# Recurrence: one joint solve of the 16x16 blocks for two units in a row, on 128 partitions

## Chip, cores, metric

One core of one Trainium2 chip. The metric is the device time of one execution in microseconds, the median of the runs.

## What is computed

The program runs two small transformer stacks one after the other on 256 tokens of width 1024, in fp32. The change lies in the second stack's first mixer, in the bidirectional recurrence over 256 context and 256 latent tokens (8 heads of 64):

```
def step(S, inp):
    r, w, k, v, kk, a = inp
    S = (S * w[:, :, None, :]
         - jnp.einsum('bhvk,bhk->bhv', S, kk)[..., None] * (kk * a)[:, :, None, :]
         + v[..., None] * k[:, :, None, :])
    return S, jnp.einsum('bhvk,bhk->bhv', S, r)
...
S_cf, y_cf = wkv7_scan(S0, dir_inputs(f_ctx, 0), reverse=False)
S_cb, y_cb = wkv7_scan(S0, dir_inputs(f_ctx, 1), reverse=True)
_, y_lf = wkv7_scan(S_cf, dir_inputs(f_lat, 0), reverse=False)
_, y_lb = wkv7_scan(S_cb, dir_inputs(f_lat, 1), reverse=True)
```

The kernel does not step token by token. It takes chunks of 64 tokens, writes a chunk's effect as a 64x64 unit triangular system per head, inverts that, and carries only the state from chunk to chunk.

## The kernel before

**Units.** The list `order` in `even_mixer` (line 1100) holds eight units: a direction `d` (0 forward, 1 backward) and a tile `t` of 128 tokens, that is two chunks of 64 tokens by 8 heads. Units 0 to 3 are the context's, 4 to 7 the latent's; even units are forward, odd ones backward. Unit 2p and unit 2p+1 together let two scan steps run.

**Steps of a unit.**
- *Front* (`rwkv_in`, lines 1449 to 1493): decays and gates from the low-rank features, products into `fr` and `gh`.
- *Back* (lines 1494 to 1545): the unit's features are loaded into `fe`, which has one buffer; VectorE scales them into `ak` and `ar`; 16 products of 128 columns go into `gg` and `gh` (line 1527), VectorE masks them into `g`. Of `g` the part that is to be inverted is stored to a DRAM buffer `dq` (line 1539), for a backward unit after VectorE's transpose (line 1537, into `fe`). Eight transposes on TensorE (line 1543) are the last readers of `fe`, with that store for a backward unit.
- *Solve* (`rwkv_solve`, lines 1555 to 1567): the 64 diagonal blocks of 16x16 (2 chunks, 8 heads, 4 blocks) are read back from `dq` with one block to a partition, tile `dl` [64, 16, 16] (line 1559). 14 rounds of a product into `dt` and a sum into `dl` (both through line 120) invert them, a fill sets the diagonal (line 1566), and the result goes to a DRAM buffer `dy` (line 1567). There are four `dq` and four `dy`, used in turn.
- *Maps* (`rwkv_maps`, lines 1569 to 1656): the solved blocks are loaded as `x` (line 1588, one load a chunk), VectorE transposes them (line 1589), and two rounds of products on TensorE (line 1594), a mask on VectorE (tile `T`) and a sum into `x` extend the 16x16 inverses to 64x64. Then come the unit's maps (lines 1636 and 1650). That is 116 calls of a product, and most of them wait for the one before by way of VectorE or ScalarE.
- *Scan steps* (`rwkv_step`, lines 1668 and 1677): after an odd unit's maps, two steps of 32 products.

**Order.** The program is written in the order of the list `GA` (line 22) and then of the loop at line 1300: `b0 s0 f1 f2 b1 f3 s1` stand among the projections before the recurrence (b is back, f front, s solve, and the number the unit); then for n from 2 on come back, front and solve of unit n, n+2 and n, then the maps of unit n-2. Softmax attention of the same mixer (`even_attention`: products into `sc`, `tr`, lines 1011, 1029, 1057) is filled in between by `fill`. Gates and readout (`gates`, `readout`) are a side stream beside the maps. A scheduler of the framework turns that into one fixed order for each engine, which waits on semaphores. All the recurrence's DMAs are issued on SP's queue.

Of the kernel before, what the change touches and what calls it, by code (L numbers as in the profile page):

```python
# [12 lines left out]
F32 = mybir.dt.float32  # L13
F32R = mybir.dt.float32r
AF = mybir.ActivationFunctionType
ALU = mybir.AluOpType
# [31 lines left out]
def kernel(ctx: ExitStack, tc: tile.TileContext, A: dict, out: bass.AP, taps=None):  # L48
    nc = tc.nc
# [8 lines left out]
    def nm(s):  # L58
        uid[0] += 1
        return f"{s}_{uid[0]}"  # L60
# [22 lines left out]
    def const(name, pool=cpool, tag=None, queue=nc.sync):  # L83
        src = A[name]
        t = pool.tile(list(src.shape), F32, tag=tag or name, name=nm(name))
        queue.dma_start(out=t, in_=src)
        return t
# [31 lines left out]
    def tt(o, a, b, op):  # L119
        V.tensor_tensor(out=o, in0=a, in1=b, op=op)  # L120
# [958 lines left out]
    def even_mixer(l, en):  # L1079
        T = 512  # L1080
        close_psum()
        with tc.tile_pool(name=nm("em"), bufs=1) as pk, tc.tile_pool(name=nm("rf"), bufs=2) as fp, \
# [9 lines left out]
            C = {n: const(n, pk) for n in ("rwkv_wa", "rtri", "gmask", "tmask", "eye2", "sgn")}  # L1092
# [7 lines left out]
            order = []  # L1100
            for i, (t0, t1) in enumerate(((2, 3), (0, 1))):
                order += [dict(d=d, t=t, u=u, i=i) for u, (d, t) in enumerate(((0, t0), (1, t1), (0, t1), (1, t0)))]
            dq = [dp.tile([64, 1040], F32, tag=f"dq{n}", name=nm("dq")) for n in range(NS)]
            dy = [dp.tile([64, 1040], F32, tag=f"dy{n}", name=nm("dy")) for n in range(NS)]
# [20 lines left out]
            with tc.tile_pool(name=nm("emn"), bufs=1) as wk:  # L1125
# [5 lines left out]
                for j in range(3):  # L1131
                    z, f = en.tile("fu", 512), en.tile("fg", 512, 2)
                    tt(z, pss[j], en.rb, ALU.mult)
                    for v in range(2):
                        c = slice(v * 256, v * 256 + 256)
# [9 lines left out]
            with tc.tile_pool(name=nm("ga"), bufs=1) as ga, tc.tile_pool(name=nm("emw"), bufs=2) as wk:  # L1145
# [100 lines left out]
                    order[u].update(next(units[u]))  # L1246

                def solve(u):
                    rwkv_solve(C, order[u])

                def do_v(f):
                    vf = shifted(8 + f)
                    stage(D["v"][:, :, f * 128:(f + 1) * 128], 4, [vf[:, t * 128:(t + 1) * 128] for t in range(4)])

                do = dict(k=do_k, q=do_q, r=do_r, v=do_v, f=front, b=back, s=solve)
                for what, n in GA:
                    do[what](n)
# [3 lines left out]
            close_half(0)  # L1261
            open_psum(gg=1, m=2, y=1, sc=1, tr=1)
            rwkv(C, D, order, (front, back, solve), bon, yac)
            for cm in reversed(held):
                cm.__exit__(None, None, None)
# [180 lines left out]
    def half(i):  # L1446
        return slice(64 * i, 64 * i + 64)
# [104 lines left out]
    def lanes_of(x):  # L1552
        return x[:, 0:1024].rearrange("l (r c) -> l r c", r=16)[:, :, 0:16]

    def rwkv_solve(C, un):
        wk = C["us"]

        y = wk.tile([64, 16, 16], F32, tag="dl", name=nm("dl"), bufs=2)
        nc.sync.dma_start(out=y, in_=lanes_of(un["dq"]))
        for c in range(1, 15):  # L1560
            n = 15 - c
            tmp = wk.tile([64, 64], F32, tag="dt", name=nm("dt"), bufs=2)
            o = tmp[:, :c * n].rearrange("p (a r) -> p a r", a=c)
            tt(o, y[:, 0:c, c].unsqueeze(2).to_broadcast([64, c, n]), y[:, c, c + 1:16].unsqueeze(1).to_broadcast([64, c, n]), ALU.mult)
            tt(y[:, 0:c, c + 1:16], y[:, 0:c, c + 1:16], o, ALU.add)
        V.memset(y.rearrange("p a r -> p (a r)")[:, 0:256:17], 1.0)
        nc.sync.dma_start(out=lanes_of(un["dy"]), in_=y)

    def rwkv_maps(C, D, un):
        d, t, u, dy, ar, g = (un[n] for n in ("d", "t", "u", "dy", "ar", "g"))  # L1570
# [213 lines left out]
    with tc.tile_pool(name="fin", bufs=1) as wk:  # L1784
# [3 lines left out]
        for k in range(0, 8, 2):  # L1788
            o = en.tile("fo", 512, 4).rearrange("p (k t) -> p k t", k=2)
# [153 lines left out]
```

## Time and profile before

| | |
|---|---|
| runs | 2334.14, 2339.14, 2340.65 us; median 2339.14 |
| profiled execution | 2338.47 us, its span 2336.7 us |
| TensorE (PE) busy | 2248.5 us, 96% |
| VectorE (DVE) busy | 1571.7 us, 67%, 3080 instructions |
| ScalarE (ACT) busy | 1073.2 us, 46% |
| mean granted TensorE clock | 0.981 |

A busy TensorE is not TensorE at its peak, since matmuls are pipelined and their ends modelled. Start times below count from the span's start. The granted clock is a share of the full 2.4 GHz. The recurrence lies between about 900 and 1175 us.

### The profile page before, as it was taken

To read this page: it belongs to the slowest core of one execution; us is meant where nothing else is said; L and a number is where in the kernel's file an instruction comes from. 1 tells how busy PE (TensorE), PEld (TensorE's weight loads), DVE (VectorE), ACT (ScalarE), POOL (GpSimd) and SP (SyncE) were. 2 spreads that over 40 slices of the span, in tenths; PEclk is the share of its full clock that TensorE was granted. 3 is DMA by queue.
4 is the path that set the end of the run, shared out by engine and by line. 5 is a ranking of instruction groups with operands and counts; after the bars stand their busy time and mean duration, and the time that the engine had idled before them with its cause. 6 is when DMAs were issued, how large, how long until landed. Compare 5 with 4: busy or idle time off the path is not lost.

```text
span 2336.7 us, 35597 instructions
## 1 busy us (share of the span) xinstructions
PE 2248.5 (96%) x13714; PEld 1842.1 (79%) x13714; DVE 1571.7 (67%) x3080; ACT 1073.2 (46%) x1887; POOL 5.6 (0%) x10
## 2 busy tenths in 40 slices
PE   8999999999999998998889999999999999999998
PEld 6688787877787786776767778787778788768998
DVE  7867778766845767889578677437755334787555
ACT  6756666322224637765535222224422223476444
POOL 0000000000000000000000000000000000000000
PEclk9999999999999999899989999999999999999999
DMA  8556545655623545433254565323553222314553
GB/s 295 174 185 209 178 149 163 190 179 159 201 95 111 172 138 142 113 88 76 77 202 146 164 190 177 129 90 121 178 189 125 91 98 92 104 37 141 184 185 119
DMA packets 161945, 342.02 MB, mean 146 GB/s; under 512 B 48624, under 2 KB 76272, under 8 KB 161648
## 3 DMA queue, kind: packets, MB, share of 16 engines
q1 hardware_dynamic: 161056, 339.15, 45.7%
q8 instruction: 108, 1.77, 0.3%
q10 hardware_dynamic: 720, 0.60, 0.1%
q14 instruction: 61, 0.50, 0.1%
HBM read 321.86 MB, written 17.84 MB: 145 GB/s over the span
## 4 chain that ended last, share of the span: by engine, by line
PE 87%; DVE 6%; ACT 4%; DMA 2%; issue 1%; SPq 0%; DVEq 0%; ACTq 0%
PE mm L115 24%; PE mm L117 24%; PE mm L116 24%; PE m L1594 1%; PE tr L219 1%; PE m L1650 1%; DVE wlo L98 1%; PE po L1057 1%; PE wm L274 1%; ACT whi L97 1%; PE wm L331 1%; PE gg L1527 1%; PE po L541 1%; DMA fe<-fd 1%; PE tr L1057 0%
## 5 line engine op out<-in xcount | busy, mean ns | idle before, releaser
L97 ACT CAST whi<-raw 128x1024 fp32r<-128x1024 f32 (+2 forms) x437 | 437.0, 1001 | 961.5 <-PE mm L116 591.4
L115 PE MATMUL mm<-xh,whi 128*128 128x512 f32 (+1 forms) x1912 | 679.2, 359 | 13.3 <-ACT xh L97 6.0
L117 PE MATMUL mm<-xh,wlo 128*128 128x512 f32 (+1 forms) x1912 | 678.6, 356 | 4.5 <-DVE wlo L98 4.3
L116 PE MATMUL mm<-xl,whi 128*128 128x512 f32 (+1 forms) x1912 | 678.6, 356 | 1.3 <-DVE xl L98 1.1
L98 DVE TENSOR_TENSOR wlo<-raw,whi 128x1024 fp32r<-128x1024 f32 (+2 forms) x437 | 508.1, 1164 | 250.5 <-ACT whi L97 244.4
L115 PEld LDWEIGHTS mm<-xh,whi 128*128 128x128 f32 x1912 | 363.4, 191 | 77.5 <-ACT whi L97 16.9
L117 PEld LDWEIGHTS mm<-xh,wlo 128*128 128x128 f32 x1912 | 364.1, 191 | 57.9 <-DVE wlo L98 8.1
L116 PEld LDWEIGHTS mm<-xl,whi 128*128 128x128 f32 x1912 | 364.5, 191 | 55.4 <-DVE xl L98 4.2
L117 PE MATMUL mm<-hh,wlo 128*128 128x512 f32 (+1 forms) x704 | 260.0, 369 | 0.0
L116 PE MATMUL mm<-hl,whi 128*128 128x512 f32 (+1 forms) x704 | 258.1, 367 | 0.1
L115 PE MATMUL mm<-hh,whi 128*128 128x512 f32 (+1 forms) x704 | 256.9, 365 | 0.0
L129 DVE SCALAR_TENSOR_TENSOR macc<-raw,modc,macc 128x1024 f32<-128x1024 f32 x189 | 234.9, 1281 | 0.5
L129 DVE SCALAR_TENSOR_TENSOR xres<-mm,mod,xres 128x256 f32<-128x256 f32 x216 | 96.3, 480 | 161.1 <-PE mm L117 160.8
L120 DVE TENSOR_TENSOR fg<-mm,fg 128x512 f32<-128x512 f32 (+1 forms) x84 | 52.4, 624 | 162.5 <-PE mm L117 162.4
L115 PEld LDWEIGHTS mm<-hh,whi 128*128 128x128 f32 x704 | 132.2, 188 | 27.6 <-ACT whi L97 2.5
L116 PEld LDWEIGHTS mm<-hl,whi 128*128 128x128 f32 x704 | 132.1, 188 | 26.1 <-DVE hl L98 0.7
L115 PE MATMUL mm<-whi,xh 128*128 128x512 f32 (+1 forms) x360 | 143.6, 403 | 8.8 <-ACT whi L97 8.3
L117 PEld LDWEIGHTS mm<-hh,wlo 128*128 128x128 f32 x704 | 132.4, 188 | 22.9
L116 PE MATMUL mm<-wlo,xh 128*128 128x512 f32 (+1 forms) x360 | 143.4, 398 | 3.0 <-DVE wlo L98 3.0
L117 PE MATMUL mm<-whi,xl 128*128 128x512 f32 (+1 forms) x360 | 141.7, 396 | 0.0
L115 PEld LDWEIGHTS mm<-whi,xh 128*128 128x128 f32 x360 | 68.5, 191 | 30.0 <-issue 9.3
L116 PEld LDWEIGHTS mm<-wlo,xh 128*128 128x128 f32 x360 | 68.9, 191 | 17.3 <-DVE wlo L98 5.3
(401 smaller groups left out, 2549.6 us busy)
## 6 DMA issues: line engine op xcount, KB each, us to landing
raw<-in_ffn_in SPq DMA_DIRECT2D x176, 512.0 KB, 3.5
raw<-in_w_mod SPq DMA_DIRECT2D x144, 512.0 KB, 4.6
raw<-in_ffn_out SPq DMA_DIRECT2D x64, 448.0 KB, 3.3
raw<-in_w_in_even SPq DMA_DIRECT2D x32, 512.0 KB, 4.8
raw<-in_w_in_odd SPq DMA_DIRECT2D x32, 512.0 KB, 3.7
raw<-in_ffn_out SPq DMA_DIRECT2D x32, 512.0 KB, 4.2
raw<-in_w_ple_gate SPq DMA_DIRECT2D x16, 512.0 KB, 3.5
raw<-in_even_r SPq DMA_DIRECT2D x15, 512.0 KB, 3.5
```

The source lines that it names most:

```text
L97: S.copy(out=hi, in_=src)
L98: V.tensor_tensor(out=lo, in0=src, in1=r32(hi), op=ALU.subtract)
L115: E.matmul(out=ps, lhsT=ah, rhs=bh, start=first, stop=False)
L116: E.matmul(out=ps, lhsT=ah, rhs=bl, start=False, stop=False)
L117: E.matmul(out=ps, lhsT=al, rhs=bh, start=False, stop=last)
L120: V.tensor_tensor(out=o, in0=a, in1=b, op=op)
L129: V.scalar_tensor_tensor(out=o, in0=a, scalar=s, in1=b, op0=op0, op1=op1)
L219: E.transpose(ps[:, j * 128:(j + 1) * 128], s, ident)
L274: E.matmul(out=ps[32 * j:32 * j + 32, hf * 256:hf * 256 + 256], lhsT=cz[:, 4 * g + j, 10 - 2 * c:42 - 2 * c], rhs=raw[:, j], start=c == 0 ...
L331: E.matmul(out=ps[32 * j:32 * j + 32], lhsT=mod_1[:, 2 - q:34 - q], rhs=acc[:, v, hf * 512:hf * 512 + 512], start=q == 0, stop=q == 2)
L541: E.matmul(out=po[:, 0:128], lhsT=pt[:, j * 128:(j + 1) * 128], rhs=vt[:, j, c], start=j == 0, stop=j == nk - 1)
L1057: E.matmul(out=po[half(a), 0:256], lhsT=vt[:, j], rhs=pt[:, j, 2 * a:2 * a + 2], start=j == 0, stop=j == nk - 1)
```

## The change

`solve` does nothing for an even unit. For an odd unit it calls `rwkv_solve` with both units of the pair. The tile `dl` gets 128 partitions, the even unit's 64 blocks in the lower half and the odd one's in the upper; two loads fill it, the 14 rounds and the diagonal's fill run once on 128 partitions, and two stores write both results.

```
                 def solve(u):
-                    rwkv_solve(C, order[u])
+                    if u % 2:
+                        rwkv_solve(C, order[u - 1], order[u])
...
-    def rwkv_solve(C, un):
+    def rwkv_solve(C, *uns):
         wk = C["us"]
 
-        y = wk.tile([64, 16, 16], F32, tag="dl", name=nm("dl"), bufs=2)
-        nc.sync.dma_start(out=y, in_=lanes_of(un["dq"]))
+        y = wk.tile([128, 16, 16], F32, tag="dl", name=nm("dl"), bufs=2)
+        for i, un in enumerate(uns):
+            nc.sync.dma_start(out=y[half(i)], in_=lanes_of(un["dq"]))
         for c in range(1, 15):
             n = 15 - c
-            tmp = wk.tile([64, 64], F32, tag="dt", name=nm("dt"), bufs=2)
+            tmp = wk.tile([128, 64], F32, tag="dt", name=nm("dt"), bufs=2)
             o = tmp[:, :c * n].rearrange("p (a r) -> p a r", a=c)
-            tt(o, y[:, 0:c, c].unsqueeze(2).to_broadcast([64, c, n]), y[:, c, c + 1:16].unsqueeze(1).to_broadcast([64, c, n]), ALU.mult)
+            tt(o, y[:, 0:c, c].unsqueeze(2).to_broadcast([128, c, n]), y[:, c, c + 1:16].unsqueeze(1).to_broadcast([128, c, n]), ALU.mult)
             tt(y[:, 0:c, c + 1:16], y[:, 0:c, c + 1:16], o, ALU.add)
         V.memset(y.rearrange("p a r -> p (a r)")[:, 0:256:17], 1.0)
-        nc.sync.dma_start(out=lanes_of(un["dy"]), in_=y)
+        for i, un in enumerate(uns):
+            nc.sync.dma_start(out=lanes_of(un["dy"]), in_=y[half(i)])
```

Line numbers behind the solve are larger by 3 after the change (1594 becomes 1597, 1650 becomes 1653), those of the back by 1.

**SP's queue at units 4 and 5.** `dq_7262` and `dq_7263` hold what units 4 and 5 are to solve, `dy_7266` and `dy_7267` what comes back, `x_2269` and `x_2209` are unit 4's loads for its maps. Before:

```order
L1559 DMA dl_10387<-dq_7263 64x16x16
L1496 DMA fe_10713<-fd 128x12x128
L1567 DMA dy_7266<-dl_10054 64x16x16
L1433 DMA K_10857<-kd 128x1024
L1435 DMA qS_10861<-qd 128x512
L1588 DMA x_2269_10831<-dy_7266 64x8x64
```

With the change:

```order
L1561 DMA dl_10253<-dq_7263 64x16x16
L1497 DMA fe_10581<-fd 128x12x128
L1378 DMA ro_9068<-lod 128x128
L1434 DMA K_10679<-kd 128x1024
L1436 DMA qS_10683<-qd 128x512
L1576 DMA lw_9041<-vd 64x4x128
L1576 DMA lw_9042<-vd 64x4x128
L1422 DMA oTd<-go_10631 128x2x128
L1570 DMA dy_7266<-dl_10253 64x16x16
L1570 DMA dy_7267<-dl_10253 64x16x16
L1591 DMA x_2209_10653<-dy_7266 64x8x64 x2
```

Unit 4's store and its loads of `x` have moved behind eight or more DMAs that follow unit 5's load; both units' stores now stand together.

**TensorE between unit 6 and unit 7.** `m` products with `lw` are the end of unit 6's maps, `m_11784` and `m_11608` the first product of unit 7's; `sc` and `tr` are attention, `y` scan steps. Before:

```order
L1650 MATMUL m_11757<-g_10730,lw_9082 128x128 x4
L1057 MATMUL tr_11844<-gpt_11638,vv_9158 64x256 x2
L1594 MATMUL m_11784<-x_2425_11778,g_11089 64x64 x16
L1057 MATMUL tr_11844<-gpt_11638,vv_9158 64x256
L1668 MATMUL y_11946<-si_9089,g_10730 64x64 x8
L1011 MATMUL sc_11995<-K_10857,qS_11633 128x256 x2
L1029 MATMUL tr_12003<-ident_63,gp_11989 128x128
L1594 MATMUL m_11802<-x_2426_11779,T_2427_11783 64x64 x16
```

With the change:

```order
L1653 MATMUL m_11574<-g_10598,lw_9038 128x128 x4
L1671 MATMUL y_11770<-si_9045,g_10598 64x64
L1653 MATMUL m_11581<-g_10598,lw_9038 128x128 x4
L1671 MATMUL y_11770<-si_9045,g_10598 64x64 x7
L1597 MATMUL m_11608<-x_2365_11602,g_10911 64x64 x16
L1597 MATMUL m_11626<-x_2366_11603,T_2367_11607 64x64 x16
L1597 MATMUL m_11651<-x_2365_11602,g_10911 64x64 x16
L1625 MATMUL m_11678<-ident_63,ar_10898 128x128 x4
```

The attention that stood among unit 7's products now stands ahead of unit 6's; unit 7's 116 calls follow one another with nothing between. Counted in TensorE's order over the whole stage, this many calls stand ahead of the first product of a unit's maps (before, then with the change):

| ahead of the maps of unit | 0 | 1 | 2 | 3 | 4 | 5 | 6 | 7 |
|---|---|---|---|---|---|---|---|---|
| attention, of 208 | 10, 26 | 40, 42 | 68, 68 | 88, 82 | 108, 121 | 126, 130 | 158, 189 | 189, 208 |
| scan steps, of 256 | 0, 0 | 0, 0 | 16, 16 | 69, 67 | 73, 128 | 136, 128 | 137, 192 | 192, 200 |
| products of the backs, of 192 | 56, 75 | 96, 96 | 104, 104 | 128, 128 | 152, 152 | 168, 180 | 192, 192 | 192, 192 |

On VectorE the 28 instructions of a joint solve stand where the odd unit's stood: the first among the instructions of unit 2's back, the second among unit 1's maps, the third among unit 3's, the last among unit 5's maps, gates and readout.

## Rows read from the trace of the kernel before

**Rows 1.** The page, part 4: the chain that ended last, by engine.
```profile
PE 87%; DVE 6%; ACT 4%; DMA 2%; issue 1%; SPq 0%; DVEq 0%; ACTq 0%
```

**Rows 2.** Stretches, by units 0, 4, 5, 6, 7: length, PE PEld DVE ACT POOL busy, clock, DMA.
```profile
939.80:973.10 33.30, 32.44 (x349) 26.57 (x349) 25.55 (x64) 22.62 (x57) 0.00 (x0) 0.81 0.45 99
...
1052.80:1084.30 31.50, 26.13 (x402) 22.29 (x400) 27.37 (x70) 15.93 (x35) 0.00 (x0) 0.95 0.29 74
1084.30:1113.80 29.50, 25.97 (x319) 19.73 (x318) 28.52 (x81) 18.20 (x32) 0.00 (x0) 1.00 0.38 94
1113.80:1140.40 26.60, 24.37 (x383) 20.30 (x382) 16.28 (x44) 14.67 (x33) 0.00 (x0) 0.94 0.36 108
1140.40:1159.20 18.80, 17.12 (x270) 14.10 (x268) 8.49 (x19) 8.84 (x21) 0.00 (x0) 1.00 0.06 17
```

**Rows 3.** Groups by line, 895 to 1190 us: the solve's instructions | busy, mean ns.
```profile
L120 DVE TENSOR_TENSOR dl<-dl,dt 64x14 f32<-64x14 f32 (+6 forms) x112 | 20.7, 185 | 0.9
L120 DVE TENSOR_TENSOR dt<-dl 64x14 f32<-64x14 f32 (+6 forms) x112 | 20.6, 185 | 1.9 <-DMA dl<-dq 0.9
```

**Rows 4.** VectorE in order of time: start, us, then the instruction.
```profile
876.05 0.23 DVE L120 TENSOR_TENSOR rpt<-ks,tab 128x64 f32<-128x64 f32 x1
```

**Rows 5.** VectorE in order of time, at solves and at maps.
```profile
924.50 0.17 DVE L120 TENSOR_TENSOR dt<-dl 64x14 f32<-64x14 f32 x1
924.70 0.17 DVE L120 TENSOR_TENSOR dl<-dl,dt 64x14 f32<-64x14 f32 x1
...
1049.60 0.70 DVE L1589 STREAM_TRANSPOSE x<-x 128x512 f32<-128x512 f32 x1
...
1074.87 0.64 DVE L120 TENSOR_TENSOR ak<-ak,fe 128x512 f32<-128x512 f32 x1
...
1092.74 0.71 DVE L1537 STREAM_TRANSPOSE fe<-g 64x512 f32<-64x512 f32 x1
...
1094.91 0.18 DVE L120 TENSOR_TENSOR dl<-dl,dt 64x36 f32<-64x36 f32 x1
1095.01 0.68 DVE L120 TENSOR_TENSOR T<-m,tmask 128x512 f32<-128x512 f32 x1
```

**Rows 6.** SP in order of time: issues of the recurrence.
```profile
921.54 0.60 SPq L1559 DMA_DIRECT2D dl<-dq  x1
...
938.62 0.59 SPq L1567 DMA_DIRECT2D dy<-dl  x1
...
1033.46 0.59 SPq L1559 DMA_DIRECT2D dl<-dq  x1
...
1057.19 0.59 SPq L1567 DMA_DIRECT2D dy<-dl  x1
1059.73 0.57 SPq L1588 DMA_DIRECT2D x<-dy  x1
...
1069.02 0.56 SPq L1496 DMA_DIRECT2D fe<-fd  x1
...
1122.46 0.59 SPq L1567 DMA_DIRECT2D dy<-dl  x1
```

**Rows 7.** The answer for line 1588, loads of x: DMA times.
```profile
DMA to landing us min/median/max: 2.6/3.4/5.4
```

**Rows 8.** Stretches of tiles sc and tr (unit 0) and m (unit 7): columns without POOL.
```profile
939.80:973.10 33.30, 2.74 (x7) 1.10 (x6) 2.69 (x4) 2.58 (x7) 0.81 0.45 99
...
939.80:973.10 33.30, 5.57 (x32) 3.25 (x32) 1.37 (x2) 1.50 (x3) 0.81 0.45 99
...
1140.40:1159.20 18.80, 12.28 (x228) 10.87 (x228) 5.02 (x8) 5.45 (x10) 1.00 0.06 17
```

**Rows 9.** Five-us stretches, columns as in the second group.
```profile
925.00:930.00 5.00, 2.07 (x8) 1.78 (x8) 3.83 (x18) 1.14 (x3) 0.00 (x0) 0.50 1.16 274
...
1070.00:1075.00 5.00, 2.20 (x37) 1.91 (x34) 3.50 (x9) 3.55 (x7) 0.00 (x0) 1.00 0.68 170
1075.00:1080.00 5.00, 4.56 (x25) 4.37 (x26) 3.87 (x15) 2.13 (x4) 0.00 (x0) 0.66 0.02 7
```

## Prediction

> **What bounds the kernel now.** I read the chain of waits first [rows 1]: TensorE holds 87% of the chain that ended last and VectorE 6%, so VectorE time is worth nothing by itself. It counts only where TensorE waits for it. The change lies inside the recurrence of the even mixer, some 270 us of the span, so I read that stage next, cut at the moments when TensorE begins a unit's maps [rows 2]. The reader is to see two regimes. While unit 0's maps run, TensorE is busy 32.44 of 33.3 us: it is short of time there, and a unit that comes later is replaced by attention and other units' products. In the stretches of units 4 and 5 VectorE is the full engine (27.37 of 31.5 us, then 28.52 of 29.5). In unit 7's stretch VectorE has 8.49 us of work in 18.8: there one unit's maps run as a chain from TensorE to VectorE or ScalarE and back, and what is left of attention fills TensorE's gaps.
>
> A unit's maps begin with the transpose of `x`, which needs the solved blocks to come back through DRAM. So the question is when each unit's solved blocks are there, against when its maps could otherwise begin.
>
> **What is removed.** Eight solves of 28 VectorE instructions become four. The 112 + 112 instructions take 20.7 + 20.6 us, 185 ns each [rows 3]; half of that is 20.65 us. The nearest instruction on 128 partitions, a product of 64 elements, took 0.23 us [rows 4], where the solve's longest rows have 56, so I price an instruction on twice the partitions as before. What a removed instruction gives back on the queue is less where other work stands between: 0.10 us from start to start (1094.91 to 1095.01), against 0.20 back to back (924.50 to 924.70) [rows 5]. A solve is thus worth 2.8 us interleaved, 5.6 us alone. The four diagonal fills that go too run beside other instructions and are put at nothing; uncovered, they are shorter than four of the solve's. The DMAs stay eight loads and eight stores; they only stand elsewhere on SP's queue. POOL's queue has nothing of this.
>
> **What is added: the even unit waits for the odd one.** The first unit of a pair now waits for the second's products, their store, their load and the joint solve.
>
> Units 0 and 1. Today unit 0's maps start at 939.8. The joint solve can begin only when unit 1's block, whose load was issued at 921.54, is there, and it should end about when unit 1's own solve does now, at 938.6 [rows 6]. From the end of a solve to a loaded `x` I count 2.5 us from a store's issue to the dependent load (1057.19 to 1059.73), 0.6 us for the second load and 3.4 us to landing [rows 6, 7]: 6.5 us, 7 with the first gap. Then come the transpose and unit 3's instructions ahead of it on VectorE, 2 to 4 us. Unit 0 starts at 948 to 950. About 1.5 us of that is saved, since unit 0's solve no longer stands among unit 1's instructions: 7 to 9 us late. By the order, 26 attention products instead of 10 and 75 products of the next units instead of 56 now stand ahead of it, and they come out of the full stretch behind it. An attention product is worth 0.21 us there (2.74 + 5.57 us for 39) [rows 8], one of the others at least the stretch's mean, 32.44 / 349 = 0.09 [rows 2]: 3.4 + 1.8 us or more come back. I carry 2 us on (bounds: 0 if all is covered, 9 if nothing is).
>
> Units 2 and 3. Unit 3's products now stand ahead of unit 0's, so its block comes early and the joint solve fits into unit 1's maps. I add nothing; the cover is unit 1's maps, and if they run faster than today up to 3 us show.
>
> Units 4 and 5. Unit 5's block is loaded from 1033.46 [rows 6], so the solve can start at 1036.5. It is interleaved with unit 3's maps, which end by 1052.8 [rows 2], so it ends near 1055; unit 5's own solve ends at 1057.19 today [rows 6]. Plus 7 us: `x` of unit 4 is transposed at 1062 instead of 1049.60 [rows 5], 12 us late. Attention (13 products more) and scan steps (55 products more) fill the gap. What follows has slack, though: unit 5 is held today by unit 7's products. Their features are loaded at 1069.02 [rows 6], used from 1074.87, transposed on VectorE until 1093.4, and unit 5's first mask product follows at 1095.01 [rows 5]. That load waits for unit 6's last use of the one buffer, which now stands right behind unit 4's first products: 1070 to 1071, 1 to 2 us late. From 1074.87 to 1092.74 some 20 solve instructions go, 2 us. So unit 5's maps begin as they do now, at +0: of the 12 us nothing is left, and the 2 us from the start are taken up by the same slack (bounds -4 and +6).
>
> Units 6 and 7. This is the term that decides. Unit 7's block is stored after 1092.74, 2.3 us ahead of unit 5's first mask product [rows 5]; its load can be issued at 1096 and land at 1099. Today unit 6 needs none of that: its maps begin at 1113.8, as soon as unit 5's are done [rows 2]. Now 28 solve instructions come first, with 26 of gates, readout, attention and unit 5 between them on VectorE: 26 x 0.6 (1095.01 has 0.68, less the overlap) + 28 x 0.11 = 18.7 us. They end near 1118, against 1122.46 for unit 7's solve today [rows 6]. Plus 7 us and the transpose: unit 6 begins near 1127 to 1128, 14 us late. Scan steps and 31 attention products are brought ahead of it, so its own stretch of 26.6 us should shrink to the 18.8 us of today's unit 7, which has the same filling [rows 2]: +6 at unit 7's start. Unit 7 then has no filling at all and saves perhaps 1 us of attention in its way.
>
> The clock. The rows show what an emptier TensorE does: 2.07 us of work in the five from 925 came with a granted 0.50, the lower of the two levels (1.2 GHz), and 2.20 in the five from 1070 with 0.66 in the next five [rows 9]. Unit 7's own products are 12.28 us of its 18.8 [rows 8], 65%, between those and the full stretches at 1.00. Without attention they cost nothing more if the clock stays, 12 us more if all of it falls, 6 for half. I take 3, nearer to no fall.
>
> A rule of the Trainium skill bears on this: "TensorE: Matmul & The Clock Gate", section Loop structure matters more than you think, says that a wait for a DMA ahead of each batch of matmuls lets the array go cold. The trace agrees at 925 (0.50), and at 1070 only the stretch behind the wait fell [rows 9]. By that rule the products behind the waits for `x` of units 0 and 6 run at the lower level too, which is the third rival's sum.
>
> **Sum** against the profiled execution (2338.47 us, span 2336.7): unit 6 +14, its stretch -8, unit 7's filling -1, the clock +3, the rest 0: **+8 us**, 2346.5. The median of the runs shown, 2339.14, is 0.7 above that execution, so I forecast **2347**. A difference of 7 us, 0.3%, is about what a measurement of this kernel can tell from no change; my forecast lies just past it.
>
> **Rivals.**
> 1. *The late units are covered.* Scan steps and attention that now run ahead of unit 6 keep TensorE busy and its clock up, and unit 7 alone is quicker than with attention in its way: the clock's 3 us go, and 3 more. For it: 19 attention products leave the last stretch. Against: with 8.49 us of VectorE there it is a chain, not a load. +2 us: 2341.
> 2. *VectorE was the bound* (the other sign). If unit 5's stretch, 28.52 us of VectorE in 29.5, is a matter of load rather than of unit 7's block, a solve less there gives 5.6 us and one less in unit 4's stretch 2.8; the joint solve then ends early and unit 6 is not late. It decides if that solve ends by 1107. -8 us: 2331. For it: rows 2. Against: the load at 1069.02 and the way of unit 7's block through DRAM are not VectorE work. The Trainium skill ("Perfetto Trace Analysis", Optimizing Scalar/DVE Operations) has grouping as the remedy where an engine is saturated, and splitting where it only causes bubbles on others; by it, unit 5's stretch would gain and the waits of units 0, 4 and 6 would be the price.
> 3. *The start is not made up.* The lower clock of unit 0's stretch (0.81 now, rows 2) lasts longer because unit 0 comes late, its 9 us are carried on, and the last units pay as in my sum: +17 or +18, 2357.
> 4. *The solve does not shrink*: on 128 partitions each instruction takes twice as long. Then the 20.65 us stay and the waits come on top: +25, 2364. Rows 4 speak against it.
>
> **Chances.** My forecast 0.45 (+3 to +13; three fifths of it past 7 us), covered 0.25, VectorE the bound 0.16, the start carried on 0.12, no shrinking 0.02. Slower by over 0.3%: 0.27 + 0.12 + 0.02 = 0.41. Faster: 0.15 of the second rival's 0.16. Within: 0.18 + 0.25 + 0.01 = 0.44. The range reaches from 2332, which takes in near half of the second rival, to 2358, the third; the bounds of the clock and of unit 5 lie inside it.
>
> **What would show it.** Right: 112 VectorE rows of 128 partitions near 0.19 us instead of 224; unit 6's maps starting near 1127; unit 7's without attention, in 17 to 22 us, at a clock below 1.00. Unit 5's first mask product near 1095 would confirm the slack behind unit 4. Wrong: unit 6 starting before 1118, unit 5 before 1090 (then VectorE bound it), or unit 4's 12 us still there at unit 5.

## The result, and the profile after

| | us, median of the runs | ratio to before (95% interval) |
|---|---|---|
| before | 2336.78 (2334.14 to 2340.65, 4 runs) | |
| the change | 2357.73 (2353.26 to 2358.73, 4 runs) | 1.0092 (1.0075 to 1.0109) |

The change costs 21 us (17.5 to 25.5), where +8 was forecast; 2357.73 lies at the upper end of the range (2358), beside the third rival's 2357 (the start not made up). The profiled execution took 2358.73 us with a span of 2356.9, 20.2 longer than before's 2336.7.

The page of the change, parts 1 and 4, which answers to [rows 1]:

```profile
PE 2259.6 (96%) x13714; PEld 1847.2 (78%) x13714; DVE 1560.4 (66%) x2964; ACT 1073.3 (46%) x1887; POOL 5.6 (0%) x10
...
PE 88%; DVE 6%; ACT 4%; DMA 2%; issue 1%; SPq 0%; DVEq 0%; ACTq 0%
```

VectorE did lose work, 11.3 us and 116 instructions against 1571.7 and 3080, and the chain of waits reads as before. So neither the load nor the chain shows the loss. The groups by line, 900 to 1200 us, answer to [rows 3] (busy us, mean ns, idle before):

```profile
L120 DVE TENSOR_TENSOR dl<-dl,dt 128x14 f32<-128x14 f32 (+6 forms) x56 | 10.9, 195 | 0.7
L120 DVE TENSOR_TENSOR dt<-dl 128x14 f32<-128x14 f32 (+6 forms) x56 | 10.9, 194 | 4.5 <-DMA dl<-dq 3.9
```

112 instructions of 195 ns stand in the place of 224 of 185: the solve shrank by 19.5 us, as priced. VectorE's total fell by less, 11.3, because the page counts time in which two instructions overlap only once.

Where the time went is seen when the stage is cut again at the first product of each unit's maps. The stretches of the change (columns as in [rows 2]), by units 0 to 7 and then the way to the next stage:

```profile
955.60:979.70 24.10, 24.10 (x295) 19.70 (x294) 16.89 (x37) 12.08 (x23) 0.00 (x0) 0.83 0.20 49
...
1030.00:1070.70 40.70, 35.85 (x452) 27.37 (x449) 31.28 (x81) 24.73 (x65) 0.00 (x0) 0.96 0.32 84
1070.70:1095.80 25.10, 20.53 (x292) 17.33 (x291) 23.69 (x45) 10.68 (x19) 0.00 (x0) 1.00 0.35 87
1095.80:1140.00 44.20, 37.89 (x461) 28.03 (x460) 32.58 (x91) 26.22 (x52) 0.00 (x0) 0.92 0.37 97
1140.00:1159.50 19.50, 17.77 (x269) 14.16 (x268) 9.36 (x20) 8.56 (x21) 0.00 (x0) 1.00 0.27 65
1159.50:1178.10 18.60, 12.59 (x230) 10.98 (x228) 9.81 (x17) 9.47 (x18) 0.00 (x0) 1.00 0.19 58
```

| start of maps of unit | 0 | 1 | 2 | 3 | 4 | 5 | 6 | 7 | end of 7 |
|---|---|---|---|---|---|---|---|---|---|
| before | 939.8 | 973.1 | 997.7 | 1025.4 | 1052.8 | 1084.3 | 1113.8 | 1140.4 | 1159.2 |
| the change | 955.6 | 979.7 | 1002.9 | 1030.0 | 1070.7 | 1095.8 | 1140.0 | 1159.5 | 1178.1 |
| later by | 15.8 | 6.6 | 5.2 | 4.6 | 17.9 | 11.5 | 26.2 | 19.1 | 18.9 |

The lateness jumps at units 0, 4 and 6, as forecast, and falls behind each. But it never falls to nothing: 4.6 us are left from the first two pairs, 11.5 at unit 5, where the forecast had none, and 18.9 at the end.

The issues on SP's queue in the change, in order of time, show the second half (they answer to [rows 6]):

```profile
1039.47 0.59 SPq L1561 DMA_DIRECT2D dl<-dq  x1
...
1061.85 1.30 SPq L1570 DMA_DIRECT2D dy<-dl  x2
1064.38 1.27 SPq L1591 DMA_DIRECT2D x<-dy  x2
...
1076.10 0.56 SPq L1497 DMA_DIRECT2D fe<-fd  x1
1077.50 0.59 SPq L1561 DMA_DIRECT2D dl<-dq  x1
...
1099.02 1.33 SPq L1540 DMA_DIRECT2D dq<-fe  x2
1102.46 0.38 SPq L1422 DMA_DIRECT2D oTd<-go  x1
1102.94 0.76 SPq L1561 DMA_DIRECT2D dl<-dq  x1
...
1127.49 1.31 SPq L1570 DMA_DIRECT2D dy<-dl  x2
1132.83 0.38 SPq L1422 DMA_DIRECT2D oTd<-go  x1
1133.30 1.27 SPq L1591 DMA_DIRECT2D x<-dy  x2
```

Unit 5's blocks are loaded at 1039.47 instead of 1033.46 [rows 6], unit 7's at 1102.94 where the forecast had 1096, and the solved blocks of units 6 and 7 leave at 1127.49, with unit 6's maps 12.5 us behind.

### The profile page after: what moved, and what is told of

It is laid out like the page before. It is cut to its first block, busy times and chain, and to the rows that moved or that the text cites. A ratio compares the mean times of both kernels' runs of the same rounds, so it can differ in the third digit from the quotient of the medians.

```text
span 2356.9 us, 35486 instructions
## 1 busy us (share of the span) xinstructions
PE 2259.6 (96%) x13714; PEld 1847.2 (78%) x13714; DVE 1560.4 (66%) x2964; ACT 1073.3 (46%) x1887; POOL 5.6 (0%) x10
## 4 chain that ended last, share of the span: by engine, by line
PE 88%; DVE 6%; ACT 4%; DMA 2%; issue 1%; SPq 0%; DVEq 0%; ACTq 0%
PE mm L115 24%; PE mm L117 24%; PE mm L116 24%; PE m L1597 1%; PE tr L219 1%; PE m L1653 1%; PE gg L1528 1%; DVE wlo L98 1%; PE po L1057 1%; PE wm L274 1%; PE tr L1057 1%; PE wm L331 1%; ACT whi L97 1%; PE po L541 1%; PE gh L1528 0%
```

## The experiments

Every kernel below was timed against the kernel before. In the table of readings at the end, "block 5" and "block 7" are the times at which the loads of unit 5's and unit 7's unsolved blocks are issued, and "end" is the issue of the first weight load behind the stage (`raw`, line 102), from SP's rows; "unit 4 transposed" is the transpose of its `x`, from VectorE's, and "unit 5's maps" the first product of these, from TensorE's. All are of the one profiled execution, which can lie up to 5 us from the median of its kernel's runs. In the cuts of code `...` stands for lines left out; in the kernels with some pairs joined these give the tile 64 or 128 partitions, by the number of units.

**Which pair costs what.** Four kernels solve one pair together and leave the other six units single; this is the one for the pair 6/7, and the number of the pair is 0, 1 or 2 in the others:

```
                 def solve(u):
-                    if u % 2:
+                    if u // 2 not in (3,):
+                        rwkv_solve(C, order[u])
+                    elif u % 2:
                         rwkv_solve(C, order[u - 1], order[u])
...
```

> Units 0 and 1 are solved together on 128 lanes; units 2 to 7 are solved singly, each in its old place. Theory A (the loss is the time for which the even unit of a pair waits for the odd one's block, and of it what its own slack does not take up): in the trace of the change unit 1 starts 6.6 us late and units 2 and 3 start 5.2 and 4.7 us late, so about +5 us (3 to 7). Rival B (the price lies in the wide work itself, its instructions, its second load and second store, so every pair costs a quarter of the 21 us): +5 us here too, and the same in the three kernels beside it. Rival C (the low granted clock at the stage's start is the loss): nearly all of the 21 us, +12 us or more.

> Units 2 and 3 are solved together; the other six singly, in their old places. Theory A: in the trace of the change units 2 and 3 do not fall further behind than unit 1 already was (6.6, then 5.2 and 4.7 us), so this pair costs nothing, -2 to +1 us. Rival B: +5 us. Rival C: 0.

> Units 4 and 5 are solved together; the other six singly, in their old places. Theory A: in the trace of the change the lateness grows from 4.7 us at unit 3 to 17.9 at unit 4 and is 11.5 at unit 5, so +7 us (5 to 9) stays. Rival B: +5 us. Rival C: 0 to 1 us. What the prediction said of this pair (the slack behind unit 7's products takes up unit 4's lateness): 0.

> Units 6 and 7 are solved together; the other six singly, in their old places. Theory A: in the trace of the change the lateness is 11.5 us at unit 5, 26.2 at unit 6, 19.1 at unit 7 and 18.9 at unit 7's end, so +7 us (5 to 9) stays. Rival B: +5 us. Rival C: 0 to 2 us.

Measured ratios: 1.0017 (1.0007 to 1.0027), 1.0007 (0.9997 to 1.0017), 0.9992 (0.9983 to 1.0002) and 1.0038 (1.0024 to 1.0051), that is about +4, +2, -2 and +9 us. A quarter each (rival B) and all at the start (rival C) both fall. But the pair 4/5 missed theory A's 5 to 9: alone it costs nothing, and the four sum to 13, not 21, each known to 2 or 3 us. The forecast's term for that pair was right where it stood alone. In that kernel unit 4 is late as forecast: VectorE's rows show it transposed at 1063.81 (forecast 1062, 1049.60 before [rows 5]). The first product of unit 5's maps and its first mask product (`T<-m,tmask`) follow:

```profile
1063.21 0.67 DVE L120 TENSOR_TENSOR g<-gg,gmask 128x512 f32<-128x512 f32 x1
1063.81 0.69 DVE L1595 STREAM_TRANSPOSE x<-x 128x512 f32<-128x512 f32 x1
...
1086.74 1.15 PE L1600 MATMUL m<-x,g 64*64 64x64 f32 x32 [0.30 <-ACT g L223]
...
1095.50 0.67 DVE L120 TENSOR_TENSOR T<-m,tmask 128x512 f32<-128x512 f32 x1
```

Unit 5 begins its maps at 1086.74, 2.4 us late, and its first mask product is half a microsecond late (1095.01 before [rows 5]); unit 6 begins at 1114.8, 1 us late. The slack is there, at the unit where the forecast put it.

**Pairs together, and the two other candidates for the price.** The same edit with two and three pairs in the list. `wide_single` solves every unit singly on 128 lanes; against the change it has

```
                 def solve(u):
-                    if u % 2:
-                        rwkv_solve(C, order[u - 1], order[u])
+                    rwkv_solve(C, order[u])
...
-        for i, un in enumerate(uns):
+        for i in range(2):
             nc.sync.dma_start(out=y[half(i)], in_=lanes_of(un["dq"]))
...
+        nc.sync.dma_start(out=lanes_of(un["dy"]), in_=y[half(0)])
```

`no_odd_work` is the kernel before without the odd units' rounds:

```
-                    rwkv_solve(C, order[u])
+                    rwkv_solve(C, order[u], u % 2)
...
-        for c in range(1, 15):
+        for c in range(1, 1 if odd else 15):
```

> Units 4 with 5 and 6 with 7 are solved together; units 0 to 3 singly, in their old places. Alone the two pairs measured -1.9 and +9.3 us, and the four pairs alone add up to +12.6 us, 8 less than the change measured. Theory A1 (the two late pairs add to each other: unit 4's late transpose on VectorE holds unit 6's and 7's last scaling, so unit 7's blocks come later, and this time unit 6 waits for them): the missing 8 us appear here, +13 to +16 us, and unit 7's blocks are loaded some 5 us later than in the kernel with 6 and 7 alone (1093.3). Theory A2 (the missing 8 us need the late start of units 0 and 1 as well): the plain sum, +6 to +9 us, with that load at 1093 to 1095. Rival B (the wide work's own price): half of 21 us, +10 us.

> Units 0 with 1, 2 with 3 and 4 with 5 are solved together; 6 and 7 singly. The three pairs alone add up to about +2.3 us (3.0, 1.2 and -1.9). Theory A1 (the missing 8 us lie between the pairs 4/5 and 6/7): +1 to +4 us. Theory A2 (they lie between the late start and the pair 4/5): +8 to +11 us. Rival B: three quarters of 21 us, +16 us.

> Every unit is solved singly in its old place, but on 128 lanes: its 64 blocks are loaded twice, into both halves of the tile, and the lower half is stored. Nothing waits for another unit, and no work is saved. Theory A: 224 instructions at 10 ns more are 2 us of VectorE, most of them beside other work: 0 to +2 us. Rival B (the price of the change lies in the wide instructions and in two loads where one was): +10 us or more.

> Units are solved singly in their old places, and the odd units' 28 multiplications and additions are left out, so that their blocks are stored as they were loaded, with ones on the diagonal; the rest is that of the kernel before. About the same VectorE work goes as in the change, and no unit waits for another. Theory A (VectorE's work is mostly beside the path that counts, its place in time is what matters): -2 to -8 us, the end of it unit 7's own solve, which goes from the stretch before unit 7. The rival of the prediction by which VectorE is the bound: -10 us or more. If the saving itself is worth -8, the wait cost the change 29 us, not 21.

Measured: 1.0062 (1.0049 to 1.0076), +14.5 us; 1.0035 (1.0022 to 1.0048), +8; 1.0001 (0.9989 to 1.0012), nothing; 0.9990 (0.9980 to 1.0000), -2. Twice the partitions and a second load cost nothing that can be measured, so rival B falls for good. And 28 solve instructions less in each of four units, with nothing made to wait, are worth 2 us (0 to 4.7): as much as can be expected of the work saved, and the rival in which VectorE was the bound (-8) falls with it. Both theories on the missing 8 us were met in part.

**The pair 4/5 taken out, the last pair again, the wait by order, the queue.** The first kernel joins all pairs but 4/5, the second is 6/7 alone once more. `single_late` is the kernel before, but writes the even unit's single solve behind the odd unit's products:

```
-                    rwkv_solve(C, order[u])
+                    if u % 2:
+                        rwkv_solve(C, order[u - 1])
+                        rwkv_solve(C, order[u])
```

`store_other_queue` is the change with attention's stores moved off SP:

```
-            nc.sync.dma_start(out=D["o"][:, 2 * kv:2 * kv + 2, q * 128:(q + 1) * 128], in_=o)
+            nc.scalar.dma_start(out=D["o"][:, 2 * kv:2 * kv + 2, q * 128:(q + 1) * 128], in_=o)
```

> All pairs are solved together but 4 and 5, which are solved singly in their old places. The change measured +21 us, the pairs 4/5 and 6/7 without the first two +14.5 (3.1 less than that interval either way), the three pairs without 6/7 +8.2, each pair alone 3.9, 1.7, -1.9 and 8.9. Theory A1 (the pair 4/5 costs nothing alone and 5 to 8 us beside the pair 6/7, since then the whole lateness of unit 7's blocks reaches the end): +13 to +16 us. Theory A2 (the pair 4/5 never costs anything; what is missing lies between the late start and the pair 6/7): +18 to +23 us.

> Units 6 and 7 alone are solved together, once more, beside the other kernels of this set: its first profile showed units 1 to 3 some 3 us earlier than the kernel before, where its program is still the same, so that chance at the stage's start may stand in its +8.9 us. From its trace, counted from the load of unit 4's blocks to the stage's end (170.0 us, against 159.1 before): +11 us; from its first median: +9 us. Theory A1 wants +7 to +9, so that 4567's +14.5 is more than this pair's own; theory A2 wants +11 to +14.

> No joint solve: the even unit's single solve stands right behind the odd unit's block, ahead of the odd unit's own, on 64 lanes each. So unit 6 (and 0, 2, 4) waits for the odd unit's block as in the change, by its place in the order, and nothing is saved. Theory A (the wait is the loss, and the change's smaller work hides a part of it): the even unit's solve is first, so it is done when the joint one would be, and the odd unit's comes 19 us behind it, for unit 7 beside unit 6's maps: +21 to +45 us. Rival B (the wide work is the price): 0 us.

> The change, with attention's small output stores (16 of 128 KB in the stage) issued from ScalarE's DMA queue instead of SyncE's. In the trace of the change such a store stands ahead of unit 7's block load (issued at 1102.46 and 1102.94) and ahead of unit 6's x (1132.83, then 1133.30, 5.8 us behind the solved blocks' store; 2.5 us is the usual distance). If SyncE's in-order queue is part of the loss, 3 to 5 us come back: +16 to +18 us against the kernel before. If the waits ahead of these loads are the blocks' own way through DRAM: +21 us as in the change.

Measured: 1.0044 (1.0029 to 1.0059), +10; 1.0051 (1.0032 to 1.0069), +12; 0.9985 (0.9971 to 0.9999), -3.5; 1.0087 (1.0068 to 1.0105), +20.

All pairs but 4/5 cost 10 us, no more than the pair 6/7 alone, below even what theory A1 expected. So the pair 4/5, free alone, is worth the other 11 us of the change beside the rest (6 to 16, from the two intervals).

The queue is not a cause that can be seen: without the store ahead of it unit 6's `x` is loaded 2.5 us behind its solved blocks (1129.45, 1131.96), as usual, and is transposed at 1139.83 all the same, against 1139.09 in the change. On VectorE attention's steps stand ahead of that transpose, and they wait for TensorE and ScalarE; in the change:

```profile
1134.24 0.42 DVE L226 COPY gpt<-tr 128x256 f32<-128x256 f32 x1 [0.94 <-PE tr L1029]
...
1137.33 0.17 DVE L1015 RECIPROCAL s<-s 128x1 f32<-128x1 f32 x1 [0.92 <-ACT gp L1014]
...
1139.09 0.71 DVE L1592 STREAM_TRANSPOSE x<-x 128x512 f32<-128x512 f32 x1
```

Unit 7's blocks came 2.7 us later there (1105.60), which the one trace doesn't explain.

`single_late` did not test what its text says. Each solve needs its own blocks alone, so in the scheduler's order the even one is not held: its rows show unit 6's solved blocks stored at 1101.33, 4 us later than before (1097.4) and 26 before the change. Unit 7's blocks are loaded 9 us earlier: 5 of them because unit 7's features are (1064.23 instead of 1069.02), and behind that unit 6's solve no longer stands among unit 7's scaling and masks:

```profile
1089.10 0.59 SPq L1561 DMA_DIRECT2D dl<-dq  x1
1101.33 0.58 SPq L1569 DMA_DIRECT2D dy<-dl  x1
```

So writing the even unit's solve later in the program is not the loss either.

**The wait alone.** `wait_only` solves each pair together, keeps the even half only, and solves the odd unit once more singly.

```
                     if u % 2:
-                        rwkv_solve(C, order[u - 1], order[u])
+                        rwkv_solve(C, order[u - 1], order[u], keep=1)
+                        rwkv_solve(C, order[u])
...
-        for i, un in enumerate(uns):
+        for i, un in enumerate(uns[:keep]):
             nc.sync.dma_start(out=lanes_of(un["dy"]), in_=y[half(i)])
```

> As in the change, the even unit's blocks are solved on 128 lanes together with the odd unit's, but only the even half is stored; the odd unit is solved once more by itself on 64 lanes, in the same place. So the even unit waits for the odd one's block through the shared tile, and none of the arithmetic is saved. Theory A (this dependency is the loss; the saved work is worth little, as the kernel without the odd units' arithmetic showed): +20 to +30 us, the change's own loss and up to 8 for the work that isn't saved. Rival D (the dependency costs little, and what costs is the changed order of the loads and stores, or that the odd unit's solve ends later): under +12 us.

Beside it ran the kernel with 2/3 and 4/5 joined:

> Units 2 with 3 and 4 with 5 are solved together; the others singly. Alone they measured +1.7 and -1.9. Theory A3 (the pair 4/5 is free only while its solve ends early, near 1052; the pair 2/3 loads unit 5's block later behind unit 4's, 25.4 us against 20.5 in its own trace, so x of unit 4 is transposed past 1064 and stands ahead of unit 6's mask products): +2 to +6 us. Theory A1 (only the pair 6/7 makes the pair 4/5 cost something): -1 to +1 us.

Measured: 1.0066 (1.0049 to 1.0083), +15 us (11 to 19); 1.0011 (0.9999 to 1.0023), +2.6. With the wait through the shared tile and none of the arithmetic saved, the kernel loses most of the change's 21 us, though less than the 20 expected, and the lower end of its interval just reaches rival D's 12. What makes the rest, some 6 us, stays open; in the traces the stage ends 5.5 us earlier than the change's (1184.30, 1189.84), of which 3.2 are there when unit 7's blocks are loaded (1099.73, 1102.94). The two solves of a pair run one behind the other, as VectorE's rows show: the single one's first round stands beside the joint one's last (the second instruction of each row). Unit 6's blocks are stored at 1121.98, unit 7's only at 1132.07 (1122.46 before), so a part of the +15 can be this lateness of the odd unit, which the change doesn't have to that extent (1127.49):

```profile
1121.02 0.24 DVE L120 TENSOR_TENSOR dt<-dl 128x14 f32<-128x14 f32 x2
...
1121.78 0.24 DVE L120 TENSOR_TENSOR dl<-dl,dt 128x14 f32<-128x14 f32 x2
```

That the even unit's wait costs by itself is plainer in the kernel with 6/7 alone: unit 6's blocks are stored 20 us later there than before (1117.78, 1097.40) and unit 7's 5 us earlier, and it is 9 to 12 us slower.

An early pair beside 4/5 gives +2.6 (-0.2 to +5.4), in theory A3's span but not clear of the other's. Its trace is of more use, below.

**A better version?** The late single solves again, and the same with 4 and 5 joined.

> The kernel that solves each unit singly, on 64 lanes, with the even unit's solve issued behind the odd unit's products, once more. It measured -3.5 us (-6.8 to -0.3), and its trace has unit 7's block loaded at 1089.10 against 1098.09 and the stage's end at 1164.60 against 1172.09. If that is the kernel's own: -2 to -7 us again. If chance at the stage's start made it: -1 to +2.

> Units 4 and 5 are solved together, as in the change; the others singly, the even unit's solve issued behind the odd unit's products. The two edits measured -1.9 and -3.5 us. If what they give lies in different stretches: -4 to -7 us. If both only load unit 7's block earlier, which is then no longer what ends the stage: -2 to -4 us.

Measured: 0.9993 (0.9982 to 1.0004) and 1.0005 (0.9995 to 1.0016). The late single solves came out 3.5 and 1.7 us below before, under the 0.3% that a measurement here can tell, and their trace has the stage's end 7.5 us earlier (1164.60; 1166.36 the second time). It is a hint, not a gain shown. Joining 4 and 5 on top shows no gain either. No version of the joint solve beats the kernel before.

**The readings side by side** (us; measured is ratio less one by 2336):

| kernel: pairs joined | measured | block 5 | unit 4 transposed | unit 5's maps | block 7 | end | end less block 7 |
|---|---|---|---|---|---|---|---|
| before: none | | 1033.46 | 1049.60 | 1084.31 | 1098.09 | 1172.09 | 74.0 |
| 0/1 | +4 | 1040.28 | 1054.84 | 1084.33 | 1100.73 | 1177.05 | 76.3 |
| 2/3 | +2 | 1037.17 | 1051.93 | 1084.47 | 1099.72 | 1175.09 | 75.4 |
| 4/5 | -2 | 1032.11 | 1063.81 | 1086.74 | 1096.97 | 1170.20 | 73.2 |
| 2/3, 4/5 | +3 | 1034.15 | 1067.24 | 1093.01 | 1103.37 | 1176.36 | 73.0 |
| 0/1, 2/3, 4/5 | +8 | 1037.98 | 1067.33 | 1093.62 | 1103.89 | 1176.05 | 72.2 |
| 6/7 | +9, +12 | 1030.13 | 1045.57 | 1077.31 | 1093.30 | 1180.12 | 86.8 |
| 4/5, 6/7 | +14.5 | 1032.23 | 1063.94 | 1086.73 | 1095.77 | 1183.86 | 88.1 |
| 0/1, 2/3, 6/7 | +10 | 1038.61 | 1055.31 | 1084.51 | 1096.99 | 1177.28 | 80.3 |
| all (the change) | +21 | 1039.47 | 1069.27 | 1095.77 | 1102.94 | 1189.84 | 86.9 |

The last column says what the pair 6/7 does: from unit 7's blocks to the end it takes 13 to 14 us more (6 in one kernel), since unit 6 now waits for them too. With 6/7 single it is 72 to 76 us, so there too the end follows unit 7's blocks, and most of what makes them late is paid in both groups. (The kernel with 6 has an execution in its profile that was 5 us faster than its median, so that figure may be chance.) The columns ahead of it say what makes them late. With 4/5 joined and no early pair, unit 4 is transposed near 1064, unit 5's maps begin 2.4 us late, and block 7 comes 1 to 2 us early. With an early pair and 4/5 single, block 5 is 4 to 7 us late, unit 4 is transposed by 1055.3, unit 5's maps begin as before, and block 7 lies between 1 us early and 3 late. Only with both is the transpose past 1067, and in all three such kernels unit 5's maps begin 8.7 to 11.5 us late and block 7 is issued 5 to 6 us late. So one slack, ahead of unit 5's maps, takes up either lateness, but not both. (The first mask product says the same but for 0/1 alone, where it is 4.6 us late, about what that kernel costs.)

How the two add up on the way to unit 7's blocks is less plain. VectorE's rows of the change, around unit 4's transpose:

```profile
1055.69 0.68 DVE L120 TENSOR_TENSOR g<-m,ar 64x512 f32<-64x512 f32 x1 [2.77 <-PE m L1653]
...
1061.63 0.18 DVE L120 TENSOR_TENSOR dl<-dl,dt 128x14 f32<-128x14 f32 x1
...
1069.27 0.70 DVE L1592 STREAM_TRANSPOSE x<-x 128x512 f32<-128x512 f32 x1
...
1071.31 0.68 DVE L120 TENSOR_TENSOR g<-gg,gmask 128x512 f32<-128x512 f32 x1
1071.91 0.67 DVE L120 TENSOR_TENSOR g<-gh,gmask 128x512 f32<-128x512 f32 x1
```

and in the kernel with 4/5 and 6/7 joined:

```profile
1052.65 0.16 DVE L120 TENSOR_TENSOR dl<-dl,dt 128x14 f32<-128x14 f32 x1
...
1060.71 0.69 DVE L120 TENSOR_TENSOR g<-gg,gmask 128x512 f32<-128x512 f32 x1 [0.76 <-PE y L1683]
...
1062.74 0.68 DVE L120 TENSOR_TENSOR g<-gh,gmask 128x512 f32<-128x512 f32 x1
1063.34 0.67 DVE L120 TENSOR_TENSOR g<-gg,gmask 128x512 f32<-128x512 f32 x1
1063.94 0.69 DVE L1595 STREAM_TRANSPOSE x<-x 128x512 f32<-128x512 f32 x1
```

The rows `g<-gg,gmask` are the masks of unit 6's own products, and the way to unit 6's blocks and to unit 7's features goes over them. In the second kernel three of the four run ahead of unit 4's transpose; in the change all four stand behind it, and the transpose itself is 5 us later, because the joint solve of 4 and 5 began later (block 5) and was held 2.8 us by an instruction of unit 3's maps ahead of it (row 1055.69). Unit 6's blocks are loaded at 1077.50 instead of 1067.95, and block 7 comes 7 us later. The order of these rows is not what counts, though. With 2/3 and 4/5 joined three of the four masks also run ahead of the transpose, and block 7 is still 5.3 us late; in `wait_only` all four stand behind it, and block 7 is 1.6 us late. The last mask ahead of the transpose and the transpose in the first, the transpose and the first mask in the second:

```profile
1066.64 0.67 DVE L120 TENSOR_TENSOR g<-gg,gmask 128x512 f32<-128x512 f32 x1
1067.24 0.69 DVE L1595 STREAM_TRANSPOSE x<-x 128x512 f32<-128x512 f32 x1
```

```profile
1064.46 0.70 DVE L1594 STREAM_TRANSPOSE x<-x 128x512 f32<-128x512 f32 x1
...
1067.65 0.68 DVE L120 TENSOR_TENSOR g<-gg,gmask 128x512 f32<-128x512 f32 x1
```

Nor does all of the lateness need unit 4's wait: with 0/1 alone unit 7's features are loaded at 1074.48, 5.5 us late, and block 7 makes up 3 of them. So what the traces show is that with both block 7 is 5 to 6 us late and with either alone 3 at most; by which instruction the one adds to the other stays open.

## Why the prediction was wrong, point by point

- **The solve's size: right.** 195 ns an instruction on 128 partitions against 185; alone, the width measured 1.0001. The fourth rival is out with it; its +25 is given without the working.
- **VectorE not the bound: right.** Saving the odd units' work with nothing waiting gave -2 us (at most 4.7); the second rival's -8 is out.
- **Units 0 and 1, "7 to 9 us late", "I carry 2 us on": mis-sized.** Unit 0 was 15.8 late. The joint solve began at 927.6, after VectorE had waited 2.04 us for unit 1's blocks to land, took 15.2 us among the instructions of unit 2's back, and ended at 942.8, not 938.6: 4.2 of the 6 to 8 us by which unit 0 missed the forecast. Behind it the transpose stood after unit 3's scaling, which waited for its features:

```profile
927.61 0.17 DVE L120 TENSOR_TENSOR dt<-dl 128x14 f32<-128x14 f32 x1 [2.04 <-DMA dl<-dq]
...
942.65 0.18 DVE L120 TENSOR_TENSOR dl<-dl,dt 128x14 f32<-128x14 f32 x1
...
949.74 0.69 DVE L120 TENSOR_TENSOR ak<-ak,fe 128x512 f32<-128x512 f32 x1 [0.55 <-DMA fe<-fd]
...
954.33 0.71 DVE L1592 STREAM_TRANSPOSE x<-x 128x512 f32<-128x512 f32 x1
```

  11.5 us lie between solve and transpose, where 7 and "2 to 4" were counted, and 1.3 more to the first product. Most came back by the cover named (unit 0's stretch is 24.1 us, 33.3 before), but 4.6 us stayed at unit 3, not 2, and joining 0/1 alone measured +4.
- **Units 4 and 5, "+0", "the 2 us from the start are taken up by the same slack": the step that failed.** Alone the pair did what was forecast (unit 5's first mask product at 1095.50, the kernel -2 us), and beside 6/7 block 7 was issued at 1095.77, where the forecast said 1096. But the slack was one for both: the forecast spent it on unit 4's 12 us and then again on the start's lateness, which was 4.8 us at unit 4's blocks and 6 at unit 5's, not 2. With both, unit 5's maps began 11.5 us late and its first mask product stood at 1100.36, so the sign that the forecast had named for being wrong (unit 4's lateness still there at unit 5) came true in the change, as it did not with 4/5 alone:

```profile
1100.36 0.68 DVE L120 TENSOR_TENSOR T<-m,tmask 128x512 f32<-128x512 f32 x1
```

  Unit 7's features were loaded at 1076.10 instead of "1070 to 1071", and block 7 was issued at 1102.94 instead of 1096.
- **Units 6 and 7, "unit 6 +14, its stretch -8": nearly right, in part by luck.** With this pair alone the joint solve's last round is at 1117.58 (forecast "near 1118"), unit 6's maps begin at 1128.4 ("1127 to 1128"), and it measured +9 and +12, where the sum had +8 with the clock's 3. But block 7 was issued at 1093.30 there, 2.7 us before the forecast's 1096, and that hid a term that was too small: from its issue to the first round it took 5.5 us (5.4 in the change), where 3 were counted. The solve itself took 19 us in both (18.7). In the change the last round came 24.5 us behind the issue, not 22, and unit 6's maps 12.5 us behind that, not 9.5, with attention's steps on VectorE in between. The shrunken stretch came as said: 19.5 (18.8).
- **The clock, +3 in unit 7's stretch: wrong, by little.** TensorE was busy 12.59 of 18.6 us there at a granted 1.00. It fell elsewhere: at unit 0, behind a stretch with 2.74 us of work in five, where the stretch's mean of 0.83 is no lower than before's 0.81, and ahead of unit 6's maps, behind five us with 2.79 of work (columns as in [rows 2]):

```profile
950.00:955.00 5.00, 2.74 (x14) 1.68 (x15) 4.51 (x9) 2.60 (x6) 0.00 (x0) 0.88 0.84 195
955.00:960.00 5.00, 5.00 (x50) 3.81 (x46) 3.64 (x7) 1.08 (x2) 0.00 (x0) 0.50 0.14 43
960.00:965.00 5.00, 5.00 (x57) 4.05 (x56) 3.42 (x8) 0.83 (x3) 0.00 (x0) 0.60 0.04 9
...
1120.00:1125.00 5.00, 2.79 (x31) 2.36 (x30) 4.56 (x14) 1.86 (x5) 0.00 (x0) 0.94 0.33 98
1125.00:1130.00 5.00, 4.53 (x47) 3.39 (x48) 2.88 (x12) 2.65 (x6) 0.00 (x0) 0.50 0.34 77
```

  The rule of the Trainium skill that the prediction weighed ("TensorE: Matmul & The Clock Gate", Loop structure matters more than you think: a long wait for a DMA between matmuls makes them run cold) thus agrees in the change with unit 0's products (0.50) and not with unit 6's and 7's, which ran at 1.00. With 6/7 alone unit 6's maps began at 1128.4, in five us at 0.59 and before five at 0.72, so there it agrees with their start too.

The sum thus misses its mark so: block 7 came 6.9 us late of the forecast, the way from it to unit 6's maps took 5.5 longer, unit 6's stretch 0.7, unit 7's 2.2 less than 20.8 (18.8, less 1 for attention, plus the clock's 3): +10.9, which is the 18.9 us at the end of unit 7 less the 8 forecast. The remaining 1.3 us of the span's 20.2 lie behind the stage. The third rival had the total (2357), but by another way: it carried unit 0's 9 us whole, and joining 0/1 alone shows that 4 are carried. That its time was met is luck.

## What to carry to other kernels

Batching two units on idle lanes makes the first wait for the second; the instructions saved can be expected to bring what a kernel that just leaves them out gains (here 2 us), and that is the first thing to measure. A slack that swallows one delay must not be counted again for the next: walk the chain of such joints from the first to the last, and ask at each what the end now waits for that it did not wait for before. A change's parts tried one by one can each look cheap or free and still cost beside the others: the pair 4/5 measured -2 us alone, and the change is 11 us slower with it than without it. So take a part out of the whole as well as trying it alone.

## What was not expected of the hardware

The same instructions can run several us apart between executions, by when the clock returns. The kernel with 6/7 joined has the kernel before's instructions in the same order on VectorE, and on TensorE as far as its rows go, until after unit 1's maps have begun, yet both its profiles have unit 1's maps begin at 970.4 and 968.5, where before has 973.1. The stretch from 940 to 950 (columns as in [rows 2]), before, then the kernel with 6/7 in its first and its second profile:

```profile
940.00:950.00 10.00, 10.00 (x66) 7.66 (x66) 4.38 (x11) 5.67 (x15) 0.00 (x0) 0.50 0.38 90
```

```profile
940.00:950.00 10.00, 10.00 (x106) 7.96 (x105) 5.97 (x14) 7.46 (x21) 0.00 (x0) 0.75 0.46 118
```

```profile
940.00:950.00 10.00, 9.36 (x116) 7.30 (x117) 7.67 (x17) 9.29 (x27) 0.00 (x0) 0.96 0.70 162
```

Behind the same stretch of a half-idle TensorE (8.8 to 9.2 us of work in the 15 us from 925, at 0.50) the granted clock is the lower level for all ten us in the one (0.50) and has come back within them in the others (0.75, 0.96). So 3 to 5 us of an early stretch in a single trace say nothing of an edit further down, and the +9, +12 and +14.5 of the kernels with 6/7 are not as far apart as they look: counted from unit 4's blocks, loaded at 1010.10 and 1014.00, to the end, 6/7 alone takes 170.0 us and 4/5 with 6/7 takes 169.9 (before: 159.1). Counted so the change takes 172.1, and it is 4.8 us late at unit 4's blocks already, so the lateness of its start reaches the end, where the kernel with all pairs but 4/5 takes 162.3.
